# Reordering the first mixer of a two-layer encoder: pooled weights split, taps on TensorE, LayerNorm sums gathered tile by tile

## The chip, the cores and the metric

One program on one core of a Trainium2 chip. The metric is the device time of one execution in microseconds (us). TensorE is called PE, its weight loads PEld, VectorE DVE, ScalarE ACT, GpSimd POOL, SyncE SP.

## The reference, cut to what matters

SEQ is 512 positions, D_MODEL 1024. Layer 0 mixes with pooling and a 31-tap convolution, layer 1 with attention; each is followed by a LayerNorm, a gated feed-forward part and a gated embedding term. Only the mixer of layer 0 is touched by the change:

```python
def pool_conv_mixer(x, w_in, pool_w, pool_scale, dw_w, dw_b, cn_g, cn_b, w_out):
    u = x @ w_in                              # 1024 -> 512 pooled + 512 value + 512 gate
    a, b_val, b_gate = u[..., :512], u[..., 512:1024], u[..., 1024:]
    # 4 groups of 128 channels, trailing windows of 2, 4, 8, 16 positions
    d = stack([window_mean(a_g, w) - a_g for g, w in ...])
    y_a = einsum('bsgc,gcd->bsgd', d, pool_w).reshape(bsz, s, 512) * pool_scale
    glu = b_val * sigmoid(b_gate)
    h = causal_dwconv(glu, dw_w, dw_b)        # 31 taps for each of 512 channels
    y_b = silu(layer_norm(h, cn_g, cn_b))     # over the 512 channels
    return concatenate([y_a, y_b], axis=-1) @ w_out
# then, in layer i:
x = layer_norm(ALPHA * x + mix, ...)
ffn = conv_ffn(x, ...)
gate = sigmoid(x @ ple_w_gate[i] + ple_b_gate[i])
x = layer_norm(ALPHA * x + ffn + gate * (p[i] @ ple_w_proj[i]), ...)
```

## The kernel before

Everything is float32. Most products are made in three passes: each operand is split into a rounded high part and the rest (`split_into`, lines 77 to 79: ACT casts, DVE subtracts), and `mm3` (lines 81 to 84) multiplies high by high, high by low and low by high in the faster fp32r format. Weights stream through the class `Weights`: SP loads a unit of 128x1024 into `wraw` (3 buffers), `split` makes `whi` and `wlo` (7 buffers).

The mixer has its channels on partitions. Eight units of `w_in` give four pairs (value, gate) of 128 channels by 512 positions (`fm_tile`). `conv` makes `glu` from a pair, and `tick` deals out the taps: some as an ACT product with a POOL addition to `h` (lines 497 to 501), the others as a DVE multiply-add into an accumulator in PSUM (lines 505 and 507). A tile closes when DVE adds both (line 512). POOL's additions read the products `pr`, of which there are 4 buffers; ACT waits for POOL when they are full.

Meanwhile PE makes the pooled channels in `group` (line 569), plain fp32 products of `xr` and `wa`, which are not split; then the embedding product `pp` of the first half with the split embedding `pth`, then `window` (lines 580 and 584), the second half of `pp`, the pooled matrix `w_pool`, and the first half of the output projection. The channel LayerNorm comes when all four tiles `h` are closed: a product with `ones` gives the mean (line 677), DVE subtracts it, ACT squares, one-column products give the variance (line 690), POOL the inverse root, a diagonal product spreads it (line 700), DVE multiplies (line 703), and ACT applies Silu.

`mix_to_gate` then finishes the output projection for the second half of the channels, token tile by token tile (`r_77` to `r_80` are the four residual tiles): `residual` adds the product to `r` (line 344), statistics follow (311 to 317), two DVE operations per half apply the norm (324 and 325), and PE transposes the tile (line 336).

A scheduler orders the instructions of the mixer and the first feed-forward part from its own estimates; each engine then runs its list in order. So an instruction that waits holds up all behind it in its engine's list.

Of the kernel before, what the change touches and what calls it, by code (L numbers as in the profile page):

```python
# [9 lines left out]
F32 = mybir.dt.float32  # L10
# [5 lines left out]
P = 128  # L16
# [23 lines left out]

NOSYNC = mybir.DependencyInfo(mybir.DependencyClass.NoSync, mybir.DependencyReason.DATA)
# [17 lines left out]
def trunk(ctx, tc, x, xt, pt, cols, w_in, w_pool, w_mo, w_qk, w_v, w_o, relb, rows, w_up, w_dn, w_pp, w_pg, out):  # L59
# [8 lines left out]
    psp = ctx.enter_context(tc.tile_pool(name="psp", bufs=4, space=PSUM))  # L68

    def psa():  # L70
        return psp.tile([P, 512], F32, tag="a", name="psa")

    def psb():
        return psp.tile([P, 512], F32, tag="b", name="psb")
# [26 lines left out]
    order = [w_in[u] for u in range(8)] + [w_pp[0], w_pp[1], w_pool] + [w_mo[u] for u in range(8)]  # L101
# [17 lines left out]
    class Weights:  # L119
# [19 lines left out]
        def split(self, cuts=None):  # L139

            raw, n = self.raw[len(self.parts)]
            hi = wp.tile([P, 1024], F32R, tag="whi", name="whi")
            lo = wp.tile([P, 1024], F32R, tag="wlo", name="wlo")
# [45 lines left out]
    def fm_tile(a):  # L189
        o = psa()  # L190
        for _ in fm_gen(o, a):
            pass
        return o
# [99 lines left out]
    wa = big.tile([P, 4, D], F32, tag="a1h", name="wa")  # L293
    A1 = [None, big.tile([P, 8, 512], F32R, name="a1l")]
# [160 lines left out]
    with tc.tile_pool(name="mix", bufs=1, reuse_waits="tile") as mp:  # L455
# [24 lines left out]
        pool.memset(ones, 1.0 / 512.0)  # L480
# [6 lines left out]
        bg, convs, hs = deque(), deque(), []  # L487

        def tap(on_pool):


            k, np_, nd, c, glu, h, acc = convs[0]
            w = col(C_DW + c * TAPS + k)
            src = glu[:, k : k + S]
            if on_pool:
                if np_ == 0:
# [5 lines left out]
                np_ += 1  # L502
            else:
                if nd == 0:
                    vec.tensor_scalar(acc, src, w, col(C_DWB + c), op0=ALU.mult, op1=ALU.add)
                else:
                    vec.scalar_tensor_tensor(acc, src, w, acc, op0=ALU.mult, op1=ALU.add)
                nd += 1
            convs[0] = (k + 1, np_, nd, c, glu, h, acc)
            if k + 1 == TAPS:  # L510
                convs.popleft()
                bg.append(lambda: vec.tensor_tensor(h, h, acc, op=ALU.add))
# [11 lines left out]
        def conv(c, pv, pg):  # L524
# [6 lines left out]
            hs.append(h)  # L531
            convs.append((0, 0, 0, c, glu, h, psb()))
# [25 lines left out]


        am = (A1[1][:, 0:4, :], A1[1][:, 4:8, :])  # L560

        def group(t):

            ts = slice(t * P, (t + 1) * P)
            o = psa()
# [50 lines left out]
        for c in range(1, 4):  # L616
# [8 lines left out]
            if c == 1:  # L625
                nc.sync.dma_start(wa[:, 0, :], w_in[8])
# [360 lines left out]
```

## Time and profile before

| | |
|---|---|
| median of 3 runs | 1257.72 us (1254.5 to 1258.06) |
| the profiled execution | 1257.47 us, of which its span is 1255.8 us |
| busy: PE, PEld, DVE, ACT, POOL | 97%, 79%, 57%, 39%, 14% of the span |
| the first 100 us alone: PE, DVE, POOL | 87.7, 88.7, 79.1 us busy |

The busy shares are means over the span. The mixer is the first 160 us or so, and there DVE and POOL are nearly as busy as PE, which they are not later.

### The profile page before, as it was taken

The page shows a single profiled execution, that of the slowest core. Times are in us where ns is not written, and L with a number is a line of the kernel's source. Part 1 is how long each engine was busy: PE and PEld are TensorE (multiplying, and loading weights), DVE is VectorE, ACT ScalarE, POOL GpSimd, SP SyncE. Part 2 cuts the span into 40 slices and gives each one's busy share as a digit, 9 for nine tenths or more (in the row PEclk, how much of TensorE's full clock was granted, in tenths as well). Part 3 has the DMA queues.
Part 4 walks back from the last instruction along what each step waited for, and adds up shares of the span by engine and source line. Part 5 has one row for each costly group of instructions (what it writes and reads, how often), then busy time and mean ns, then how long its engine had stood idle before and what let it go on. Part 6 is the DMA issues. An engine that isn't in the chain of part 4 may idle for free.

```text
span 1255.8 us, 14245 instructions
## 1 busy us (share of the span) xinstructions
PE 1221.9 (97%) x5478; PEld 995.9 (79%) x5478; DVE 716.9 (57%) x1043; ACT 491.2 (39%) x745; POOL 175.6 (14%) x183
## 2 busy tenths in 40 slices
PE   8989999999999999999989999979999999999997
PEld 6638878888888888888878888868888888888886
DVE  7996586543444344447457777595544344434427
ACT  6764333431333133313357776222432233223320
POOL 5990040000000000004013233140000000000001
PEclk9999999999999999999999999999999999999999
DMA  9321123332222322333322222122322222223201
GB/s 364 137 67 67 51 101 107 129 101 101 93 92 101 101 94 90 101 101 101 134 84 76 96 82 67 67 101 85 134 91 94 101 101 98 87 101 101 96 22 67
DMA packets 36643, 125.11 MB, mean 100 GB/s; under 512 B 4064, under 2 KB 4448, under 8 KB 36576
## 3 DMA queue, kind: packets, MB, share of 16 engines
q1 hardware_dynamic: 36576, 124.20, 29.0%
q8 instruction: 43, 0.70, 0.2%
q14 instruction: 24, 0.20, 0.0%
HBM read 122.09 MB, written 2.10 MB: 99 GB/s over the span
## 4 chain that ended last, share of the span: by engine, by line
PE 86%; DVE 5%; POOL 5%; issue 2%; ACT 1%; DMA 1%; SPq 0%; DVEq 0%; POOLq 0%; ACTq 0%
PE psa L82 22%; PE psa L83 22%; PE psa L84 22%; PE psb L83 5%; PE psb L82 5%; PE psb L84 5%; POOL h L501 4%; PE psb L834 2%; DVE r L325 1%; DVE r L324 1%; PE psb L803 1%; PE psb L852 1%; PE psb L851 1%; PE psb L802 1%; POOL s L822 1%
## 5 line engine op out<-in xcount | busy, mean ns | idle before, releaser
L79 DVE TENSOR_TENSOR wlo<-wraw,whi 128x1024 fp32r<-128x1024 f32 (+3 forms) x191 | 239.3, 1254 | 328.7 <-ACT whi L78 322.6
L78 ACT CAST whi<-wraw 128x1024 fp32r<-128x1024 f32 (+2 forms) x203 | 211.8, 1043 | 460.9 <-PE psa L83 229.0
L82 PE MATMUL psa<-a0h,whi 128*128 128x512 f32 x896 | 351.0, 393 | 2.4 <-ACT whi L78 1.2
L84 PE MATMUL psa<-a0h,wlo 128*128 128x512 f32 x896 | 349.4, 390 | 2.0 <-DVE wlo L79 2.0
L83 PE MATMUL psa<-a0l,whi 128*128 128x512 f32 x896 | 349.6, 390 | 0.0
L82 PEld LDWEIGHTS psa<-a0h,whi 128*128 128x128 f32 x896 | 168.8, 188 | 38.4 <-ACT whi L78 2.2
L84 PEld LDWEIGHTS psa<-a0h,wlo 128*128 128x128 f32 x896 | 168.7, 188 | 38.2 <-DVE wlo L79 2.8
L83 PEld LDWEIGHTS psa<-a0l,whi 128*128 128x128 f32 x896 | 168.8, 188 | 34.7 <-DVE a0l L79 0.4
L319 POOL TENSOR_TENSOR rs<-ve,nhalf 128x1 f32<-128x1 f32 x16 | 15.0, 937 | 505.7 <-DVE ve L317 505.7
L411 DVE TENSOR_TENSOR hr<-t,psa 128x512 f32<-128x512 f32 x44 | 30.3, 689 | 86.0 <-PE psa L84 83.1
L501 POOL TENSOR_TENSOR h<-h,pr 128x512 f32<-128x512 f32 x47 | 71.1, 1526 | 6.0 <-ACT pr L500 3.7
L822 POOL TENSOR_TENSOR s<-s,rc 128x512 f32<-128x512 f32 (+1 forms) x64 | 47.8, 779 | 155.9 <-DVE rc L818 117.1
L82 PE MATMUL psa<-whi,a0h 128*128 128x512 f32 x160 | 63.7, 398 | 0.0
L82 PE MATMUL psa<-whi,a1h 128*128 128x512 f32 x160 | 63.0, 394 | 0.0
L83 PE MATMUL psb<-wlo,a1h 128*128 128x512 f32 x160 | 63.0, 394 | 0.0
L82 PE MATMUL psb<-whi,a1h 128*128 128x512 f32 x160 | 62.9, 393 | 0.0
L408 ACT ACTIVATE t<-t 128x512 f32<-128x512 f32 x44 | 27.9, 633 | 89.1 <-DVE t L407 89.1
L84 PE MATMUL psa<-whi,a0l 128*128 128x512 f32 x160 | 62.6, 391 | 0.0
L83 PE MATMUL psa<-wlo,a0h 128*128 128x512 f32 x160 | 62.5, 391 | 0.0
L83 PE MATMUL psa<-wlo,a1h 128*128 128x512 f32 x160 | 62.3, 389 | 0.0
L84 PE MATMUL psb<-whi,a1l 128*128 128x512 f32 x144 | 56.1, 398 | 0.0
L84 PE MATMUL psa<-whi,a1l 128*128 128x512 f32 x144 | 55.9, 389 | 0.0
(196 smaller groups left out, 1744.6 us busy)
## 6 DMA issues: line engine op xcount, KB each, us to landing
wraw<-in_w_up SPq DMA_DIRECT2D x88, 512.0 KB, 3.5
wraw<-in_w_dn SPq DMA_DIRECT2D x44, 512.0 KB, 3.5
wraw<-in_w_pg SPq DMA_DIRECT2D x16, 512.0 KB, 3.5
wraw<-in_w_qk SPq DMA_DIRECT2D x16, 512.0 KB, 3.5
wraw<-in_w_mo SPq DMA_DIRECT2D x8, 512.0 KB, 3.5
wraw<-in_w_v SPq DMA_DIRECT2D x8, 512.0 KB, 3.5
bt<-in_relb SPq DMA_DIRECT2D x16, 256.0 KB, 2.6
wraw<-in_w_o SPq DMA_DIRECT2D x8, 512.0 KB, 3.6
```

The source lines that it names most:

```text
L78: act.copy(hi, src)
L79: eng.tensor_tensor(lo, src, hi.bitcast(F32), op=ALU.subtract)
L82: pe.matmul(o, lhsT=ah, rhs=bh, start=first, stop=False)
L83: pe.matmul(o, lhsT=ah, rhs=bl, start=False, stop=False)
L84: pe.matmul(o, lhsT=al, rhs=bh, start=False, stop=last)
L319: pool.tensor_tensor(rs, ve, nhalf, op=ALU.pow)
L324: vec.scalar_tensor_tensor(r[t][:, c], r[t][:, c], mv[:, 0:1], self.g[:, c], op0=ALU.subtract, op1=ALU.mult)
L408: act.activation(t, t, AF.Gelu_apprx_tanh)
L411: vec.tensor_tensor(hr, t, pv, op=ALU.mult)
L501: pool.tensor_tensor(h, h, pr, op=ALU.add)
L822: pool.tensor_tensor(s[:, c], s[:, c], rc[:, b : b + 1].broadcast_to([P, n]), op=ALU.mult)
L834: pe.transpose(bank[:, n : n + P], s[:, SO[b] + j * P : SO[b] + (j + 1) * P], ident)
```

## The change

What is computed stays the same. In the order of the program:

- `make_bands` is issued ahead of the products; the Silu table is loaded once by a tiny activation.
- The four pooled units of `w_in` come through `Weights` and are split into `wa[0]` and `wa[1]`; `group` uses three passes, with the already split input `A0`.
- Taps 0 and 1 of each tile are products of PE with a diagonal matrix `dt` that ACT makes (`seed`); DVE then adds its taps to that accumulator.
- For tiles 2 and 3 `seed` also subtracts the channel mean of tile 0 with a product by `nmean`; `shift` does it for tiles 0 and 1 afterwards.
- The windows come right behind the groups, then `w_pool`, then half of the output projection's first half; the embedding product comes behind these.
- The LayerNorm's sums of `h` and of its square are one-column products made tile by tile (`sums`) between pieces of the embedding product. Mean and inverse root are both spread by diagonal products, and DVE multiplies and subtracts.
- The PSUM banks go by three tags (`a` and `c` with 2, `b` with 4).

```diff
-    order = [w_in[u] for u in range(8)] + [w_pp[0], w_pp[1], w_pool] + [w_mo[u] for u in range(8)]
+    order = [w_in[u] for u in range(12)] + [w_pool, w_mo[0], w_mo[1], w_pp[0], w_pp[1]] + [w_mo[u] for u in range(2, 8)]
...
+        def seed(n):
+            c, glu = n["c"], n["glu"]
+            n["acc"] = bank("c")
+            for k in range(PE_TAPS):
+                d = mp.tile([P, P], F32, tag="dt", name="dt", bufs=2)
+                act.activation(d, ident, AF.Copy, scale=col(C_DW + c * TAPS + k))
+                last = k == PE_TAPS - 1 and c < 2
+                pe.matmul(n["acc"], lhsT=d, rhs=glu[:, k : k + S], start=k == 0, stop=last)
+            if c >= 2:
+                pe.matmul(n["acc"], lhsT=nmean, rhs=hs[0], start=False, stop=True)
+            if c == 3:
+                bg.append(lambda: shift(0))
...
+        def close(n):
+            c, h = n["c"], n["h"]
+            vec.scalar_tensor_tensor(h, h, col(C_DWB + c), n["acc"], op0=ALU.add, op1=ALU.add)
+            hs.append(h)
+            if c == 1:
+                shift(1)
+
+        def shift(c):
+            sh = bank("a")
+            pe.matmul(sh, lhsT=nmean, rhs=hs[0], start=True, stop=True)
+            vec.tensor_tensor(hs[c], hs[c], sh, op=ALU.add)
...
             for k in range(KD):
-                lhs = xr[k // 2][:, H[k % 2]][:, ts]
-                pe.matmul(ov, lhsT=lhs, rhs=wa[:, :, k * P : (k + 1) * P], start=k == 0, stop=k == KD - 1)
-            split_into(am[0][:, t, :], am[1][:, t, :], o)
+                ks = slice(k * P, (k + 1) * P)
+                mm3(ov, A0[0][:, k, ts], A0[1][:, k, ts], wa[0][:, :, ks], wa[1][:, :, ks], k == 0, k == KD - 1)
+            a = mp.tile([P, 2, S], F32R, tag="pp", name="am", bufs=4)
+            split_into(a[:, 0, :], a[:, 1, :], o)
...
+        def sums(c):
+            sq = mp.tile([P, S], F32, tag="sg", name="sq", bufs=2)
+            act.activation(sq, hs[c], AF.Square)
+            for n, a in enumerate((sq, hs[c])):
+                for t in range(NT):
+                    i = n * NT + t
+                    pe.matmul(
+                        pvr[:, i : i + 1],
+                        lhsT=a[:, t * P : (t + 1) * P],
+                        rhs=mcol,
...
-        for c in range(4):
-            vec.tensor_tensor(hs[c], hs[c], pm, op=ALU.subtract)
...
+        both = []
+        for n in range(2):
+            if n:
+                vec.tensor_tensor(mean, mean, rs, op=ALU.mult)
+            dg = mp.tile([P, S], F32, tag="sg", name="dg", bufs=2)
+            v = mean if n else rs
...
         for c in range(4):
-            vec.tensor_tensor(hs[c], hs[c], rstd, op=ALU.mult)
+            vec.tensor_tensor(hs[c], hs[c], both[0], op=ALU.mult)
+            vec.tensor_tensor(hs[c], hs[c], both[1], op=ALU.subtract)
```

Three places in the engines' lists. The first is the start of the taps on DVE, in the kernel before from the first `glu` on:

```order
L529 TENSOR_TENSOR glu<-psa,sg 128x512
L505 TENSOR_SCALAR psb<-glu,cst 128x512
L507 SCALAR_TENSOR_TENSOR psb<-glu,cst,psb 128x512 x3
L79 TENSOR_TENSOR wlo<-wraw,whi 128x1024
L507 SCALAR_TENSOR_TENSOR psb<-glu,cst,psb 128x512 x2
```

And in the changed one:

```order
L578 TENSOR_TENSOR glu<-psa,sg 128x512
L88 TENSOR_TENSOR wlo<-wraw,whi 128x1024
L543 SCALAR_TENSOR_TENSOR psc<-glu,cst,psc 128x512
L88 TENSOR_TENSOR wlo<-wraw,whi 128x1024
L543 SCALAR_TENSOR_TENSOR psc<-glu,cst,psc 128x512 x5
```

Four taps that stood between `glu` and the first split now stand behind it, since they add to a bank that PE's seed fills.

The second is DVE around the windows in the changed kernel (`am` are the split group results, `a1l` on `psa`, `psb` the split windows, L553 a closing tile, L561 a shift):

```order
L543 SCALAR_TENSOR_TENSOR psc<-glu,cst,psc 128x512 x2
L88 TENSOR_TENSOR am<-psb,am 128x512
L553 SCALAR_TENSOR_TENSOR h<-h,cst,psc 128x512
L543 SCALAR_TENSOR_TENSOR psc<-glu,cst,psc 128x512
L561 TENSOR_TENSOR h<-h,psa 128x512
L543 SCALAR_TENSOR_TENSOR psc<-glu,cst,psc 128x512 x3
L88 TENSOR_TENSOR am<-psb,am 128x512
L543 SCALAR_TENSOR_TENSOR psc<-glu,cst,psc 128x512
L88 TENSOR_TENSOR a1l<-ptr,a1h 128x512 x2
L543 SCALAR_TENSOR_TENSOR psc<-glu,cst,psc 128x512 x2
L561 TENSOR_TENSOR h<-h,psa 128x512
L543 SCALAR_TENSOR_TENSOR psc<-glu,cst,psc 128x512 x4
```

The next row is the first split window, so eleven taps stand between the split of the third group and that of the first window. In the kernel before the embedding product and its splits stood between groups and windows.

The third is DVE in `mix_to_gate`, before:

```order
L344 SCALAR_TENSOR_TENSOR r_78<-r_78,psa 128x512
L315 BN_AGGR mv<-st 128x2
L311 BN_STATS st<-r_78 128x6
L317 TENSOR_SCALAR ve<-mv 128x1
L324 SCALAR_TENSOR_TENSOR r_77<-r_77,mv,g 128x512 x2
L315 BN_AGGR mv<-st 128x2
L325 SCALAR_TENSOR_TENSOR r_77<-r_77,rs,b 128x512 x2
```

And in the changed kernel:

```order
L357 SCALAR_TENSOR_TENSOR r_78<-r_78,psa 128x512
L324 BN_STATS st<-r_77 128x6
L324 BN_STATS st<-r_78 128x6
L328 BN_AGGR mv<-st 128x2 x2
L330 TENSOR_SCALAR ve<-mv 128x1
L337 SCALAR_TENSOR_TENSOR r_77<-r_77,mv,g 128x512 x2
L330 TENSOR_SCALAR ve<-mv 128x1
L337 SCALAR_TENSOR_TENSOR r_78<-r_78,mv,g 128x512 x2
L357 SCALAR_TENSOR_TENSOR r_79<-r_79,psc 128x512
L338 SCALAR_TENSOR_TENSOR r_77<-r_77,rs,b 128x512 x2
```

The last step of `r_77`, for which PE's transposes wait, now stands behind work on `r_78` and behind the residual of `r_79`. The PE list behind these transposes is the same in both kernels, and so are the lists of the feed-forward parts and the attention.

## Rows read from the trace of the kernel before

**Rows 1.** The page: span, busy time, the chain that ended last.

```profile
span 1255.8 us, 14245 instructions
PE 1221.9 (97%) x5478; PEld 995.9 (79%) x5478; DVE 716.9 (57%) x1043; ACT 491.2 (39%) x745; POOL 175.6 (14%) x183
PE 86%; DVE 5%; POOL 5%; issue 2%; ACT 1%; DMA 1%; SPq 0%; DVEq 0%; POOLq 0%; ACTq 0%
```

**Rows 2.** PE's waits from 0 to 200 us: total, times, longest.

```profile
PE psa L82 <- DVE a1l L79: 4.4, 2, 3.5
PE psa L336 <- DVE r L325: 2.4, 1, 2.4
...
PE psa L84 <- DVE wlo L79: 2.0, 2, 1.2
PE psa L82 <- ACT whi L78: 1.2, 1, 1.2
...
PE psa L84 <- DVE pth L79: 0.7, 2, 0.5
```

**Rows 3.** Stretches: length, busy per engine, granted clock, DMA share, GB/s.

```profile
94.40:102.40 8.00, 8.00 (x50) 7.68 (x51) 8.00 (x12) 3.29 (x5) 1.42 (x2) 0.79 0.07 17
...
126.00:130.00 4.00, 4.00 (x12) 3.14 (x13) 1.04 (x5) 0.00 (x0) 1.02 (x1) 0.57 0.00 0
...
174.10:178.00 3.90, 3.87 (x14) 3.45 (x15) 3.87 (x8) 2.44 (x3) 0.93 (x1) 0.56 0.15 56
```

**Rows 4.** DVE's groups by shape, 20 to 110 us.

```profile
L507 DVE SCALAR_TENSOR_TENSOR psb<-glu,cst,psb 128x512 f32<-128x512 f32 x69 | 48.4, 748 | 0.3
L79 DVE TENSOR_TENSOR wlo<-wraw,whi 128x1024 fp32r<-128x1024 f32 x13 | 22.6, 1739 | 4.8 <-ACT whi L78 4.8
```

**Rows 5.** DVE in order of time: start, length, what, how many.

```profile
20.62 0.81 DVE L505 TENSOR_SCALAR psb<-glu,cst 128x512 f32<-128x512 f32 x1
...
47.96 1.21 DVE L79 TENSOR_TENSOR wlo<-wraw,whi 128x1024 fp32r<-128x1024 f32 x1
...
94.23 4.70 DVE L507 SCALAR_TENSOR_TENSOR psb<-glu,cst,psb 128x512 f32<-128x512 f32 x7
98.84 0.68 DVE L512 TENSOR_TENSOR h<-h,psb 128x512 f32<-128x512 f32 x1
...
105.92 0.69 DVE L512 TENSOR_TENSOR h<-h,psb 128x512 f32<-128x512 f32 x1
```

**Rows 6.** POOL in order of time, its first additions.

```profile
22.05 62.08 POOL L501 TENSOR_TENSOR h<-h,pr 128x512 f32<-128x512 f32 x39 [3.25 <-ACT pr L500]
```

**Rows 7.** PE in order of time, to the end of the groups.

```profile
24.73 0.39 PE L83 MATMUL psa<-a0l,whi 128*128 128x512 f32 x1
25.86 0.50 PE L84 MATMUL psa<-a0h,wlo 128*128 128x512 f32 x1 [0.73 <-DVE wlo L79]
...
40.13 0.39 PE L82 MATMUL psa<-a0h,whi 128*128 128x512 f32 x1
...
55.79 27.63 PE L569 MATMUL psa<-wa,xr 128*128 128x512 f32 x64
```

**Rows 8.** PE in order of time, the longest wait and the one-column products.

```profile
94.37 0.50 PE L82 MATMUL psa<-whi,pth 128*128 128x512 f32 x1 [3.54 <-DVE a1l L79]
...
122.93 3.18 PE L690 MATMUL psa<-ones,sq 128*128 128x1 f32 x28
```

**Rows 9.** ACT in order of time, its first table load.

```profile
0.79 1.28 ACT L475 ACT_TABLE_LOAD   x1 [0.79 <-PEq L979]
```

**Rows 10.** DVE in order of time, in `mix_to_gate`.

```profile
155.07 0.69 DVE L344 SCALAR_TENSOR_TENSOR r<-r,psa 128x512 f32<-128x512 f32 x1
...
157.90 1.36 DVE L325 SCALAR_TENSOR_TENSOR r<-r,rs,b 128x512 f32<-128x512 f32 x2
```

**Rows 11.** PE in order of time, the first and the third transposed tile.

```profile
158.65 1.32 PE L336 MATMUL psa<-ident,r 128*128 128x128 f32 x8
...
174.13 1.97 PE L336 MATMUL psa<-ident,r 128*128 128x128 f32 x8 [2.37 <-DVE r L325]
```

More of the change, by code (lines that the diff above doesn't have):

```diff
@@ L1 @@
 from collections import deque
-from itertools import chain
+from itertools import chain, cycle
 import concourse.bass as bass
@@ L623, in trunk @@
             conv(c, pv, pg)
[L624 to L627 removed]
+        ptr = mp.tile([P, 2, S], F32, name="ptr")
+        nc.sync.dma_start(ptr, pt[0].rearrange("p (k t) -> p k t", k=2))
         for t in range(NT):
             nc.sync.dma_start(r[t], x[t * P : (t + 1) * P, :])
+        eps_t2 = sm.tile([P, 1], F32, tag="e2", name="eps_t2", bufs=1)
+        for _ in POOLED:
+            W.take()
+            W.free()
         for t in range(NT):
             group(t)
+            if t == 0:
+                act.activation(eps_t2, eps_t, AF.Silu)
             tick(*TICK)
@@ L652, in trunk @@
+            W.free()
+            if h == 0:
+                while bg or convs:
+                    tick(2, 1)
+                for c in range(min(3, len(hs)), 4):
+                    pass
             W.pump()
-            if h == 0:
-                A1[0] = big.tile([P, 8, 512], F32R, tag="a1h", name="a1h")
-                for g in range(NW):
-                    window(g)
         W.auto = True
-        while bg or convs:
-            tick(2, 1)
-        y = A1[:]
-        wpl = W.take()
@@ L691, in trunk @@
-        ve = sm.tile([P, NT], F32, tag="nm", name="ve4")
-        vec.tensor_scalar(ve, pvr[:, :NT], EPS, None, op0=ALU.add)
+        done = 3
+        for c in range(done, 4):
+            sums(c)
+        mean = sm.tile([P, NT], F32, tag="nm", name="mean")
+        vec.tensor_copy(mean, pvr[:, NT : 2 * NT])
+        sqm = sm.tile([P, NT], F32, tag="sqm", name="sqm")
+        vec.scalar_tensor_tensor(sqm, mean, -1.0, mean, op0=ALU.mult, op1=ALU.mult)
+        ve = sm.tile([P, NT], F32, tag="ve4", name="ve4")
@@ L693, in trunk @@
+        vec.scalar_tensor_tensor(ve, pvr[:, :NT], EPS, sqm, op0=ALU.add, op1=ALU.add)
         rs = sm.tile([P, NT], F32, tag="rc", name="rs4")
         pool.tensor_tensor(rs, ve, nhalf.broadcast_to([P, NT]), op=ALU.pow)
-        next(first)
-        dg = mp.tile([P, S], F32, tag="sg", name="dg", bufs=2)
-        for t in range(NT):
-            vec.tensor_scalar(dg[:, t * P : (t + 1) * P], ident, rs[:, t : t + 1], 512.0, op0=ALU.mult, op1=ALU.mult)
-        rstd = psa()
-        pe.matmul(rstd, lhsT=ones, rhs=dg, start=True, stop=True)
@@ L701, in trunk @@
-        next(first)
+        both = []
[4 more added lines that the diff above has]
+            v = mean if n else rs
+            for t in range(NT):
+                vec.tensor_scalar(dg[:, t * P : (t + 1) * P], ident, v[:, t : t + 1], None, op0=ALU.mult)
+            b = bank("c")
+            pe.matmul(b, lhsT=ones, rhs=dg, start=True, stop=True)
+            both.append(b)
```

178 lines of the change are left out of this document (102 added, 76 removed).

## The prediction

> **What bounds the kernel now.** I read the page first, then PE's waits, then DVE and POOL in order of time in the mixer. PE is busy for 97% of the span and holds 86% of the chain that ended last [rows 1], so outside the mixer time is PE work, and the lists behind the mixer are equal in both kernels. Only the first 180 us can differ. There PE waits in four places [rows 2]: 3.2 us for weights being split (2.0 for DVE, 1.2 for ACT), 5.1 us at the embedding product (4.4 for the split group results, 0.7 for `pth`), and 2.4 us in `mix_to_gate` for `r_79`. PE slows behind a long wait: the granted clock is 0.79 over the 8 us behind the wait of 3.54, and 0.56 behind the wait of 2.37 [rows 3, 8, 11]. It is also 0.57 behind the one-column products [rows 3]. The full clock is 2.4 GHz, the lower level 1.2. What PE waits for is DVE, which from 20.62 to its last closing tile at 105.92 has almost no gap [rows 5].
>
> **PE's work.** A product of 512 columns in fp32r takes (55.79 - 40.13) / 69 = 0.227 us [rows 7], with 69 products between the two rows. In plain fp32 it shows as two records of 27.63 / 64 = 0.432, so 0.864 [rows 7].
> - Groups: 32 fp32 products (27.6) become 96 at 0.227 (21.8): -5.8.
> - Eight diagonal products: +6.9. Four products with `nmean`: +3.5. The mean's four products with `ones` go: -3.5. A second spreading product: +0.9.
> - One-column products: 16 become 32. One is two records, and 28 of those take 3.18 [rows 8], so 0.22 each: +3.5.
>
> The sum is +5.5 us: PE gets more work, not less. Windows, embedding product, `w_pool` and output projection keep their counts.
>
> **DVE's work up to the last closing tile.** A tap takes (98.84 - 94.23) / 7 = 0.66 [rows 5]. Of 124 taps before, DVE did 73; of 116 it now does 67, and POOL 45 additions for 47: -4.0. The four splits of pooled weights come on top. A 1024-column split takes 1.21 alone [rows 5], but in the mean of this stretch 1.74 [rows 4], so +7.0 by the mean; the bounds are 4.8 (always alone) and 9.7 (each waits as long as it runs). Two shifts add 1.3. The scheduler also puts ahead of the last closing tile the four subtractions behind `w_pool` (2.6) and two splits (2.4) that stood behind it. At the start, DVE's first tap waits for the seed, which on PE stands behind unit 2 of `w_in`. That unit ends at 25.0 [rows 7], so the seed's 1.7 us end near 26.6. DVE, which began its taps at 20.62 [rows 5], has only one split to do until then: about 4 us idle, some 3 of which it spent idle further on before, so +1. In all 105.9 - 4.0 + 7.0 + 1.3 + 2.6 + 2.4 + 1 = 116 for the last closing tile, 10 us later. PE reaches the sums of the fourth tile only near 122, so this in itself costs nothing: the embedding product and half of the output projection cover it.
>
> At one place the Trainium skill speaks against the change. The row shows a split of 1.21 alone and 1.74 on average beside POOL's additions [rows 4, 5]. The page "SBUF — State Buffer", section "Who interferes with whom", says that a DVE instruction with two SBUF inputs and a GpSimd one that reads SBUF share a port under an exclusive lock, so that the later one is fully blocked. By it each of the four new splits could at worst wait for a whole addition, and blocks additions as well. The mean in the rows lies between that and no contact, and the sum goes by the mean.
>
> **PE in order of time in the changed kernel.** The early waits go: ACT's cast of unit 5 now stands behind 10 products instead of 13, and POOL's pace of 62.08 / 39 = 1.59 per addition [rows 6] sets when these can be made. PE starts the groups at 55.8 - 3.2 + 3.5 (two seeds) + 0.3 = 56.4. The 0.3 is for a second table load at the start: one takes 1.28 [rows 9], most of it before the first inputs; bounds 0 and 1.3.
>
> Groups (21.8), the third seed and three `nmean` products (4.3) and the first window pieces (0.8) bring PE to 83.3. It then needs the second and third group split. DVE has by then to do, from 20.6: 4.2 idle, 15 splits (26.1) and a half one (1.1), 41 taps (27.1), and seven short operations at about 0.6 (4.2); that gives 83.3, and some 84.8 with the dearer early taps, since the mean over all is 0.75 [rows 4]. A wait of 1 to 2 us.
>
> Behind it PE does the last seed, `nmean` and the other windows in 7.4 us, to about 92.2. DVE needs for the eleven taps (7.3) and seven short operations (4.3) 11.6 us until the first split window, 96.4, and 3.1 more until the fourth (two taps, three splits), 99.5. PE has 14 products (3.2) for that time. So PE passes this place at 99.6 instead of 83.3 + 7.4 + 3.2, with 5.7 us of waits in all. What is late next is `w_pool`'s results, but the embedding product and tile-by-tile order fill that.
>
> The half clock behind these waits falls partly into the next wait; I take 0.8 (bounds 0 and 1.7, the latter from 0.21 of 8 us [rows 3]) against the 1.7 that go with the old wait.
>
> To the first transposes: +5.5 - 3.2 - 5.1 - 1.7 + 5.7 + 0.3 + 0.8 = +2.3.
>
> **`mix_to_gate`.** Before, DVE had `r_77` ready as PE came to its transposes at 158.65 (residual of `r_78` at 155.07, last step of `r_77` at 157.90 [rows 10, 11]). Now two statistics, both first norm steps of `r_78` and the residual of `r_79` stand ahead of that last step. From the end of `r_78`'s sums, 12 products (2.7 us) ahead of the transposes: 0.25 to start, residual 0.6, two statistics 1.2, aggregation and epsilon 0.4, four norm steps 2.7, residual 0.6, one last step 0.7 = 6.4. So PE waits 6.4 - 2.7 = 3.7. In return `r_79` is ready in time: its steps end some 12 us after the first transposes would have started and PE wants it some 16 to 19 after. The wait of 2.4 goes [rows 11], and the half clock moves from one place to the other. Net +1.3.
>
> **Sum.** 2.3 + 1.3 = +3.6 on the profiled 1257.5 of which 1255.8 is span; the LayerNorm's half clock (0.43 of 4 us = 1.7 [rows 3]) may or may not go, since the one-column products now come in pieces of under 2 us: I take a third of it as gained, -0.6. Hence +3.0. The profiled execution and the median of 1257.7 differ by 0.2; the forecast is **1260.5 us**. A difference under 0.3%, 3.8 us, is what a measurement of this kernel cannot tell from none.
>
> **The rivals.**
> 1. *The waits go altogether* (faster). If collisions with POOL cost little, 15 splits at 1.21 instead of 1.74 bring DVE 8 us forward: both waits at the windows (5.7) and their half clock (0.8) vanish, and the LayerNorm's too (1.1 more): 1260.5 - 7.6 = 1253. For it: POOL has two additions fewer. Against: rows 4. It decides from a mean split of 1.4.
> 2. *ACT holds the group results back* (slower). ACT's casts of the last three group results stand behind products that wait for POOL; the second is behind 41 of them, so behind addition 37, at 22 + 37 x 1.59 = 81, in time. Four more splits than before hold POOL too. At 1.75 per addition the third cast, behind addition 38, comes at 88.5 and its split at 89.5, 4.7 after the 84.8 above, and the windows, their splits and all behind move by that: 1265. With the half clock in full at both new waits (2.6), 1267. It decides from 1.65 per addition.
> 3. *The seeds do not free DVE*: that DVE's work does not fall is already in the sum. Were the seed's four microseconds of idle time fully made up by shorter queues later, it would be -3: 1257.5, no change.
>
> Chances: the forecast with its neighbour 3, within 1255 to 1264.5, 0.50; rival 1 in part or whole 0.21; rival 2 in part or whole 0.29. The range that leaves out 2 in 10 is 1253 to 1267. The forecast stands close to the 0.3% border at 1261.5, so of its half I put 0.36 within and 0.14 above; with a small part of the rivals: faster 0.20, same 0.42, slower 0.38.
>
> **What would show it right or wrong.** In the changed profile: group products at 0.227; PE starting them near 56 with no waits for `whi` or `wlo`; PE waiting for `am` and `a1l` near 85 and 95, in all about 6 us; the last closing tile near 116 with no PE wait behind it; a wait of 3 to 4 us at the transposes of `r_77` and none at `r_79`. Wrong would be a mean split clearly off 1.74, POOL's pace off 1.6, or `r_77` in time.

## The result, and the profile after

The changed kernel takes 1272.18 us (median of 4, 1270.3 to 1272.39) against 1257.89 for the kernel before beside it: a ratio of 1.0115, 95% interval 1.0093 to 1.0136. It is slower by some 14 us, where 3 were forecast and 1267 was the upper end of the range. The page of the profiled execution (span, busy time of the engines, shares of the chain that ended last):

```profile
span 1270.4 us, 14431 instructions
...
PE 1234.9 (97%) x5560; PEld 1012.6 (80%) x5560; DVE 723.6 (57%) x1050; ACT 496.8 (39%) x757; POOL 177.7 (14%) x183
...
PE 86%; POOL 5%; DVE 4%; ACT 1%; issue 1%; DMA 1%; SPq 0%; DVEq 0%; POOLq 0%
```

Beside [rows 1], PE is busy for 13 us more and the span is 14.6 longer; POOL holds as much of the chain as before. PE's waits in the first 220 us (engine, what it does at which line, what it waits for, total, times, longest):

```profile
PE psb L491 <- ACT warm L488: 3.9, 1, 3.9
PE psc L519 <- DVE h L553: 3.8, 1, 3.8
PE psa L632 <- DVE h L561: 3.6, 1, 3.6
PE psc L349 <- DVE r L338: 3.5, 1, 3.5
PE psa L560 <- DVE am L88: 1.5, 1, 1.5
PE psb L92 <- DVE a1l L88: 0.3, 1, 0.3
```

Of [rows 2], the waits for split weights, for `pth` and for `r_79` are gone, as forecast. Three of 3.5 to 3.8 us stand in their place: for tile 0's closing (L553) ahead of the third tile's diagonal products, for a shift (L561) ahead of the fourth window, and for `r_77`. Behind each of them the granted clock is low (the 0.65, 0.57 and 0.72 near the end of each row; PE is hardly idle in these stretches):

```profile
69.00:77.00 8.00, 7.56 (x15) 3.79 (x16) 6.50 (x7) 6.10 (x9) 7.69 (x5) 0.65 0.50 187
101.00:109.00 8.00, 7.70 (x25) 5.76 (x26) 8.00 (x13) 5.02 (x9) 0.00 (x0) 0.57 0.00 0
172.00:178.00 6.00, 5.99 (x23) 4.74 (x24) 6.00 (x11) 2.61 (x4) 2.08 (x2) 0.72 0.00 0
```

That costs 0.35 x 8 + 0.43 x 8 + 0.28 x 6 = 7.9 us, and 8.5 with a first row that holds its stretch whole (from 66 on). Before there were two such stretches behind waits, 3.4 us in all [rows 3]. The one behind the one-column products, 1.7 us, is there in both kernels.

From the start of the span to the first feed-forward activation the kernel before takes 222.14 us and the changed one 232.85. PE's time splits into three parts: idle (length less busy), time lost to the lower clock (length times what the granted clock lacks to 1), and the rest, which I call work. The rows for all but the first 20 us, of before:

```profile
20.00:222.14 202.14, 191.03 (x796) 144.19 (x795) 157.76 (x211) 99.29 (x138) 86.02 (x56) 0.97 0.32 110
```

and of after:

```profile
20.00:232.85 212.85, 200.20 (x881) 159.58 (x880) 164.67 (x218) 103.92 (x148) 88.01 (x54) 0.95 0.30 105
```

The first 20 us add 3.5 and 3.9 of idle time at full clock. Over 200 us a clock of two digits is good to 1 us only, so the lost part in this table, and in what follows, is summed from narrow windows, each around one stretch at the lower level:

| to the first feed-forward activation | idle | lost to the clock | work | sum |
|---|---|---|---|---|
| before | 14.6 | 5.1 | 202.4 | 222.1 |
| after | 16.5 | 10.2 | 206.1 | 232.8 |
| forecast of the difference | -1.0 | -1.5 | +5.5 | +3.0 |
| measured difference | +1.9 | +5.1 | +3.7 | +10.7 |

Another 3.6 us come behind it: from that activation to the last `hr` of the last feed-forward part, before takes 982.7 us and after 986.3, with the same products in the same order. Split in the same way, these 3.6 us are 2.4 of work, 1.7 lost to the clock and -0.5 of idle time.

### The profile page after: what moved, and what is told of

Same layout as the page of the kernel before. It is cut to its first block, busy times and chain, and to the rows that moved or that the text cites. A ratio compares the mean times of both kernels' runs of the same rounds, so it can differ in the third digit from the quotient of the medians.

```text
span 1270.4 us, 14431 instructions
## 1 busy us (share of the span) xinstructions
PE 1234.9 (97%) x5560; PEld 1012.6 (80%) x5560; DVE 723.6 (57%) x1050; ACT 496.8 (39%) x757; POOL 177.7 (14%) x183
## 4 chain that ended last, share of the span: by engine, by line
PE 86%; POOL 5%; DVE 4%; ACT 1%; issue 1%; DMA 1%; SPq 0%; DVEq 0%; POOLq 0%
PE psa L91 11%; PE psa L92 11%; PE psa L93 11%; PE psc L91 11%; PE psc L93 11%; PE psc L92 11%; PE psb L92 5%; PE psb L93 5%; PE psb L91 5%; POOL h L540 4%; PE psb L923 2%; PE psb L892 1%; PE psb L940 1%; PE psb L941 1%; PE psb L891 1%
## 5 line engine op out<-in xcount | busy, mean ns | idle before, releaser
L88 DVE TENSOR_TENSOR wlo<-wraw,whi 128x1024 fp32r<-128x1024 f32 (+2 forms) x191 | 239.0, 1253 | 341.8 <-ACT whi L87 335.4
L87 ACT CAST whi<-wraw 128x1024 fp32r<-128x1024 f32 (+1 forms) x203 | 211.4, 1042 | 464.9 <-PE psb L93 118.5
L91 PE MATMUL psa<-a0h,whi 128*128 128x512 f32 x440 | 174.3, 396 | 0.0
L92 PE MATMUL psa<-a0l,whi 128*128 128x512 f32 x440 | 172.4, 392 | 0.0
L93 PE MATMUL psa<-a0h,wlo 128*128 128x512 f32 x440 | 172.2, 391 | 0.0
L91 PE MATMUL psc<-a0h,whi 128*128 128x512 f32 x416 | 162.5, 391 | 0.0
L93 PE MATMUL psc<-a0h,wlo 128*128 128x512 f32 x416 | 162.0, 389 | 0.0
L92 PE MATMUL psc<-a0l,whi 128*128 128x512 f32 x416 | 161.9, 389 | 0.0
L92 PEld LDWEIGHTS psa<-a0l,whi 128*128 128x128 f32 x440 | 83.2, 189 | 17.7 <-DVE a0l L88 0.4
L93 PEld LDWEIGHTS psa<-a0h,wlo 128*128 128x128 f32 x440 | 83.2, 189 | 17.5
```

Of the source, the lines that this page charges most:

```text
L87: act.copy(hi, src)
L88: eng.tensor_tensor(lo, src, hi.bitcast(F32), op=ALU.subtract)
L91: pe.matmul(o, lhsT=ah, rhs=bh, start=first, stop=False)
L92: pe.matmul(o, lhsT=ah, rhs=bl, start=False, stop=False)
L93: pe.matmul(o, lhsT=al, rhs=bh, start=False, stop=last)
```

## The experiments

Ratios are to the kernel before on the same chip; the changed kernel's is 1.0115, and 0.0010 is 1.26 us.

### What is lost behind the mixer

**e4_tags.** Two PSUM tags in the kernel before.

```diff
-        return psp.tile([P, 512], F32, tag="a", name="psa")
+        return psp.tile([P, 512], F32, tag=next(turns), name="psa")   # turns = cycle("aacc"), 2 banks each
```

> The kernel before, with one part of the change alone: the four PSUM banks of tag a become two of tag a and two of tag c taken in the order a, a, c, c. Behind the mixer the changed kernel lost 3.6 us more although its lists there are the same but for these tags. Theory A (the tags cost nothing, and what was lost behind the mixer has another cause): 1256 to 1260, no change. Theory B (the two rings make PE wait later on in the feed-forward parts or the attention): 1261 to 1263.

Ratio 1.0056 (1.0038 to 1.0075), slower as theory B has it, but not where B has it: 8.6 us are lost in the mixer and 2 to 3 regained later. With two tags the scheduler puts PE's transposes of `r_77` behind the last tile's part of the output projection and those of `r_78` right behind them:

```profile
168.73 1.11 PE L337 MATMUL psa<-ident,r 128*128 128x128 f32 x4 [3.89 <-DVE r L326]
171.49 1.11 PE L337 MATMUL psa<-ident,r 128*128 128x128 f32 x4 [1.64 <-DVE r L326]
```

The DVE steps that these wait for take 5.58 us for two, beside two weight splits on POOL; apart from such splits two take 1.36 [rows 10]:

```profile
165.85 5.58 DVE L326 SCALAR_TENSOR_TENSOR r<-r,rs,b 128x512 f32<-128x512 f32 x2
```

```profile
165.65 5.24 POOL L80 TENSOR_TENSOR wlo<-wraw,whi 128x1024 fp32r<-128x1024 f32 x2
```

In the changed kernel the transposes stand a product tile apart, as before. So the tags are a way to lose time, not the way in which it was lost here.

**e5_align and e12_before_moved.** In e5 the changed kernel's displacement of 160 bytes is made 256, a multiple of 128; in e12 the kernel before is given the 160.

```diff
-        eps_t2 = sm.tile([P, 1], F32, tag="e2", name="eps_t2", bufs=1)    # e5, in the changed kernel
+        eps_t2 = sm.tile([P, 32], F32, tag="e2", name="eps_t2", bufs=1)
...
+        pool.memset(sm.tile([P, 40], F32, tag="pad", name="pad", bufs=1), 0.0)    # e12, in the kernel before
```

> The changed kernel with one small tile made 128 bytes long instead of 4, so that everything allocated behind it in SBUF moves by 96 bytes per partition; no instruction changes. In the changed kernel the operand tiles hh and hl of the feed-forward parts' middle chunk start 160 bytes further on than before, at a multiple of 32 bytes and no longer of 128, and their products follow each other every 0.2343 us instead of 0.2289; 384 products make 2.1 us. Theory A (the address makes the difference): 0.2289 again, and the time falls by 2 to 3 us, to about 1269.5. Theory B (the banks psb and psc that they write, or DVE's work beside them, make it): still 0.2343, and 1271 to 1273.

> The kernel before with a small unused tile of 160 bytes ahead, so that the tiles behind it start where they start in the changed kernel: hh and hl of the feed-forward parts at a multiple of 32 bytes and not of 128. Lists of instructions are the same but for one short POOL instruction at the start. Theory A (the addresses cost what the changed kernel lost behind the mixer): their products at 0.2343 us instead of 0.2289, and the time rises by 2 to 4 us, to 1259 to 1261. Theory B (the spacing comes from something else in the changed kernel): 0.2289, no change.

e5: 1.0076 (1.0052 to 1.01), 4.9 us less than the changed kernel, whose interval it just touches. e12: 1.0039 (1.0024 to 1.0053), 4.9 us more than the kernel before, and its whole interval lies above 1. Theory A both times, by more than it said. Products of `hh`, start and length; first before, 32 products apart, (431.58 - 424.26) / 32 = 0.2288 us each:

```profile
424.26 0.39 PE L83 MATMUL psa<-wlo,hh 128*128 128x512 f32 x1
...
431.58 0.39 PE L82 MATMUL psa<-whi,hh 128*128 128x512 f32 x1
```

In the changed kernel, also 32 apart, 0.2341:

```profile
424.28 0.40 PE L92 MATMUL psb<-wlo,hh 128*128 128x512 f32 x1
...
431.77 0.40 PE L91 MATMUL psb<-whi,hh 128*128 128x512 f32 x1
```

In e12, 31 apart, 0.2345, with the instructions of before:

```profile
424.49 0.40 PE L82 MATMUL psb<-whi,hh 128*128 128x512 f32 x1
...
431.76 0.40 PE L83 MATMUL psa<-wlo,hh 128*128 128x512 f32 x1
```

384 such products make some 2 us. From the first feed-forward activation to the last `hr`, e5 takes 982.4 us (before 982.7) and e12 985.6 (after 986.3). But not all of this is the addresses. PE's work in that part is 971.1 to 972.1 us in the eight kernels with `hh` where the changed kernel has it and 968.1 to 969.3 in the ten with `hh` at a multiple of 128, e10 among them; the time lost to the clock there is 1.7 to 5.1 us in both groups, 5.1 in e10. The clock near 660 us (third number from the right) shows it, in the kernel before, in the changed one, and in e10:

```profile
650.00:670.00 20.00, 19.17 (x97) 16.46 (x98) 11.74 (x26) 13.44 (x32) 5.93 (x10) 0.91 0.24 78
```

```profile
650.00:670.00 20.00, 16.98 (x71) 14.04 (x70) 10.86 (x29) 12.84 (x29) 4.04 (x6) 0.83 0.24 82
```

```profile
650.00:670.00 20.00, 16.93 (x79) 14.31 (x78) 10.27 (x29) 11.60 (x27) 6.67 (x10) 0.83 0.25 72
```

So of the 3.6 us behind the mixer the addresses are some 2.4, and 1.7 is a clock that does not go with them. Over all executions, spans times granted clocks differ by 3.0 us between e12 and the kernel before and by 3.4 between the changed kernel and e5 (estimates from the span and clock of each execution; the second pair ran on different chips). So some 3 of the 4.9 us are shown to be the addresses; that the rest, lost to the clock, is theirs too is not shown.

**e16_moved64.** e12 with 16 elements in place of 40.

> The kernel before with an unused tile of 64 bytes ahead, so that hh and hl start at 64 bytes past a multiple of 128, where all the other operands of these products start (whi, wlo, a0h, a0l, a1h, a1l). Theory A (only starts that are no multiple of 64 cost): products of hh at 0.2289 us or less, and 1254 to 1258, no change. Theory B (only a multiple of 128 is good): products above 0.2289, and the time between the kernel before and the one moved by 160 bytes, 1258 to 1261. Theory C (what counts is that both operands start at the same place within 128 bytes): 0.2266, and 1 us faster.

0.999 (0.9974 to 1.0007): no difference in time that can be told, which fits theory A and the 1 us of theory C. The products go as theory C says, 31 apart, 0.2268:

```profile
424.64 0.39 PE L82 MATMUL psa<-whi,hh 128*128 128x512 f32 x1
...
431.67 0.39 PE L83 MATMUL psa<-wlo,hh 128*128 128x512 f32 x1
```

### What is lost in the mixer

**e2_bank.** The fourth window in a bank that needs no shift to be read.

```diff
-            o = [pse() for _ in range(NW)]
+            o = [pse() for _ in range(NW - 1)] + [bank("b")]
```

> The changed kernel, with the fourth window in a PSUM bank of tag b, so that it no longer waits for the bank that the spreading product of tile 0's mean holds until DVE has read it (a PE wait of 3.6 us at 97.3 us). Theory A (the bank alone holds PE there): the wait is gone, the first w_pool product starts 3 to 4 us earlier, and with the half clock behind it the time falls by 4 to 5 us, to 1267 or 1268. Theory B (DVE and ACT are late by themselves, so that the split windows come no earlier): PE waits as long a little further on, for a1h or a1l, and the time falls by at most 1 us, 1271 to 1272.

1.0116 (1.0096 to 1.0137): no gain, theory B. The wait of 3.6 is gone, and PE waits for `am` and `a1h` instead, starting `w_pool` at 101.9 instead of 102.5:

```profile
88.59 2.00 PE L560 MATMUL psa<-h,nmean 128*128 128x512 f32 x2 [2.66 <-DVE am L88]
...
101.92 0.50 PE L91 MATMUL psa<-a1h,whi 128*128 128x512 f32 x1 [2.76 <-ACT a1h L87]
```

**e3_noshift and e6_seedbank.** Two ways to free the third tile's products: e3 leaves out all products with `nmean` and both shifts (unshifted variance), e6 gives the accumulator another bank.

```diff
-            if c >= 2:                                                    # e3
-                pe.matmul(n["acc"], lhsT=nmean, rhs=hs[0], start=False, stop=True)
...
-            n["acc"] = bank("c")                                          # e6
+            n["acc"] = bank("b" if c == 2 else "c")
```

> The changed kernel without the subtraction of tile 0's mean: four products with nmean (3.5 us of PE) and two DVE additions (1.4 us) go, the LayerNorm takes its variance from unshifted sums. Theory A (the third tile's diagonal products wait for DVE to close tile 0 because they take over the PSUM bank of its accumulator): the wait of 3.8 us at 65.7 stays within 1 us, the wait of 3.6 for the fourth window goes, and the time falls by 3.5 (products) and some 2 to 3 (wait, half clock), to about 1266. Theory B (they wait because their third product reads tile 0 itself): both waits go, with the half clock behind them, and the time falls by about 10 us, to 1262.

> The changed kernel, with the third tile's diagonal products written to a PSUM bank of tag b, so that they need not wait until DVE has closed tile 0 (a PE wait of 3.8 us at 65.7, and half clock behind it). They still wait for tile 0 through the product with nmean, which can stand later in PE's list. Theory A (PE's wait is a loss of its own): the wait is gone, and with the half clock behind it the time falls by 4 to 6 us, to about 1267. Theory B (the windows are held back by DVE and ACT, which do not get earlier): PE waits longer for am and a1h near 90 to 100, and only the half clock is gained: 1270 to 1272.

e3: 1.0142 (1.0119 to 1.0164), no gain although 3.5 us of PE are gone; both theories had less. The wait at the diagonal products stays, as theory A says (the bank holds them), PE waits longer for other things, `r_77` among them, and 13.7 us are lost to the clock, 3.4 more than in the changed kernel:

```profile
PE psc L349 <- DVE r L338: 5.2, 1, 5.2
...
PE psc L519 <- DVE h L549: 3.8, 1, 3.8
```

e6: 1.0089 (1.0066 to 1.0112). Its interval overlaps the changed kernel's, so the 3 us may be chance; and the wait is not gone, as theory A had it. The diagonal products come early, and the product with `nmean` behind them waits as long for the same closing:

```profile
56.15 1.88 PE L519 MATMUL psb<-glu,dt 128*128 128x512 f32 x4
...
69.58 1.74 PE L521 MATMUL psb<-h,nmean 128*128 128x512 f32 x2 [3.78 <-DVE h L553]
```

So bank and data both tie the third tile to tile 0's closing at 68.65, and to take one away is not enough.

**e7_pr6.** Six buffers of `pr` (the raw embedding moves into another tile to make room).

```diff
-                    pr = mp.tile([P, S], F32, tag="pr", name="pr", bufs=4)
+                    pr = mp.tile([P, S], F32, tag="pr", name="pr", bufs=6)
```

> The changed kernel with six buffers of products pr instead of four, so that ACT can run further ahead of POOL's additions (ACT waits 18.8 us for POOL between 20 and 130 us, and DVE 9.3 us for casts that stand behind these products on ACT). Theory A (ACT held by POOL is what makes the windows late): DVE's idle time for whi falls below 5 us, the windows come 3 to 5 us earlier, and the time falls by 2 to 5 us, to about 1268.5. Theory B (POOL's pace of 1.68 us per addition is the limit, and two more buffers only move the place where ACT waits): ACT's wait and the time stay, 1271 to 1273.

1.0111 (1.0084 to 1.0138): no gain, theory B. ACT's wait falls only to 12.6 us, from 18.8, and POOL's 45 additions take 75.4 us as in the changed kernel. Tile 0 closes at 60.3, so the third tile's products run without a wait, but PE then waits 6.4 us in one piece for `am` (the profiled execution is 4.9 us below this kernel's median):

```profile
61.22 1.88 PE L519 MATMUL psc<-glu,dt 128*128 128x512 f32 x4
...
85.34 2.07 PE L560 MATMUL psa<-h,nmean 128*128 128x512 f32 x2 [6.44 <-DVE am L88]
```

**e8_noseed and e9_noseed_pr6.** No products of PE for taps or mean (unshifted variance): `PE_TAPS = 0`, DVE's first tap with the bias as before, the closing a plain addition. e9 adds e5's and e7's edits.

> The changed kernel without any products of PE for the taps: no diagonal products, no product with nmean (12 products, 10.4 us of PE), all 31 taps again by DVE or ACT and POOL, and the LayerNorm's variance from unshifted sums. DVE gets 8 taps more and 2 additions less (+4 us), and starts its taps some 4 us earlier. Theory A (PE's list sets the time once the waits for the seeds are gone): the time falls by 8 us or more, to 1264 or less. Theory B (DVE's list up to the windows and the last closing tile sets it): PE waits longer at the windows, and the time falls by less than 4 us, to 1268 to 1274.

> The changed kernel with three edits together: no products of PE for the taps and the mean shift (unshifted variance), six buffers of pr, and the tiles behind the small pool at a multiple of 128 bytes again. What stays of the change: pooled weights split, new order of windows and embedding product, channel LayerNorm from gathered sums, PSUM tags. Theory A (the three losses are separate: 5 us for the seeds, 6 for ACT behind POOL, 4 to 5 for the addresses): the feed-forward part starts near 222 as before, and the time is 1255 to 1260. Theory B (seeds and pr buffers act on the same wait, PE's for the split group results, so that their gains overlap): a wait of 4 us or more for am stays, and the time is 1261 to 1265.

e8: 1.0083 (1.0062 to 1.0105), 4 us less than the changed kernel, with intervals that overlap; the median of 1266.9 lies between the theories. Of work it has some 193 us, 13.1 less, but 21.1 idle and 13.7 lost to the clock: PE waits 7.1 us for ACT's cast of `am` and then runs slowly (third number from the right):

```profile
80.00:100.00 20.00, 15.75 (x62) 13.64 (x63) 16.56 (x26) 16.12 (x27) 19.29 (x15) 0.58 0.06 23
```

e9: 1.0082 (1.006 to 1.0103), no less than e8. PE still waits 7.7 us for `am`, as theory B says, but the median of 1267.3 is above B's range too: 23.9 idle, 20.5 lost to the clock. Much of the work taken from PE comes back as waits and clock.

**e10_seedbank_pr6.** e5, e6 and e7 together.

> The changed kernel with three edits together: the third tile's diagonal products in a bank of tag b, six buffers of pr, and the tiles behind the small pool at a multiple of 128 bytes. Theory A (the gains of 3 us in the mixer for the bank, 6 for the buffers and 4 for the addresses add): first feed-forward activation near 224, time 1258 to 1260. Theory B (with six buffers tile 0 is closed in time, so that the bank gives nothing more): first feed-forward activation near 226.5, time 1262 to 1265.

1.0039 (1.0021 to 1.0056), 9.5 us less than the changed kernel; the median of 1261.3 lies between the theories. Its profile is of the longest of 12 executions, 4.9 us above the median; in it the first feed-forward activation comes at 228.5, later than either theory has it, with 14.4 us idle and 8.5 lost to the clock. With e9 it shows that the diagonal products are worth having: e9 is e10 without them and without the product with tile 0's mean, and 5 us slower, although it has some 16 us less of PE's work; 12 us of that come back as lost clock and 9.5 as idle time.

**e14_plain.** e10 with the pooled weights unsplit: plain products of `xr` and `wa`, as in the kernel before, and splits of the windows behind the last window product.

> The kernel of e10 with the pooled products undone: plain fp32 products of unsplit weights (27.6 us of PE instead of 21.8), no casts and splits of the four pooled units; the split windows must wait for the last window product, since the group results lie where they go. Theory A (the splits of the pooled weights, 7 us of DVE, cost at PE's waits and half clock behind them about what the faster products give): within 2 us of e10, 1259 to 1263. Theory B (PE's work sets the time, as in the prediction's sum): 4 to 6 us slower than e10, 1265 to 1267.

1.0119 (1.0097 to 1.0142), 10 us slower than e10; both theories had less. Up to the feed-forward part work rises by 4.4 us, as in theory B, and the loss to the clock by 3.4 to 12.0, of which 9 lie in one stretch:

```profile
100.00:120.00 20.00, 19.27 (x74) 17.33 (x75) 13.41 (x20) 7.60 (x12) 0.00 (x0) 0.55 0.12 42
```

So the split groups pay, and DVE's four splits are not where the loss lies. Part of the 10 us may be the later splits of the windows, which this version needs.

**e11_before_pr6.** The kernel before with six buffers.

> The kernel before with six buffers of pr instead of four (half of the split embedding is kept in another tile for that, with no other change). Theory A (ACT held by POOL's additions, 17.3 us of waits, is behind PE's waits for weights and for the embedding product, 3.2 and 5.1 us): at least half of these go, and the time falls by 3 to 6 us, to 1252 to 1255. Theory B (in the kernel before DVE is late by itself): no change, within 2 us.

1.0016 (1.0 to 1.0032): no gain here either, theory B.

### The end of the mixer

**e1_order.** In `mix_to_gate` the residual of a tile stays behind the last norm step of the tile before.

```diff
             residual(t, 1, by.o[t], True)
+            if t:
+                tc.add_manual_dep(ins[n], last[t - 1], NOSYNC, reason="written order")
```

> The changed kernel, with one dependence added on DVE's list in mix_to_gate: the residual of a token tile may not stand ahead of the last norm step of the tile before it, so r_77's last step no longer stands behind the work on r_78 and the residual of r_79. Theory A (PE waits at the transposes of r_77, 3.5 us and some half clock behind it, because of that order): the wait shrinks to about 1 us, and the time falls by 2.5 to 4 us, to about 1269. Theory B (the wait only moves, to the transposes of r_78 or r_79): a wait of 2 us or more for r_78 or r_79 appears, and the time changes by under 1 us, 1271 to 1273.

1.0122 (1.0103 to 1.0141): no gain, theory B. PE waits 0.6 us for `r_77` and 3.8 for `r_79`, the tile behind `r_78`:

```profile
169.43 0.66 PE L349 MATMUL psc<-ident,r 128*128 128x128 f32 x4 [0.61 <-DVE r L338]
...
186.77 0.63 PE L349 MATMUL psc<-ident,r 128*128 128x128 f32 x4 [3.83 <-issue]
```

The reason is on DVE: the last steps of `r_78` take 5.70 us where those of `r_77` took 1.40,

```profile
168.63 1.40 DVE L338 SCALAR_TENSOR_TENSOR r<-r,rs,b 128x512 f32<-128x512 f32 x2
...
174.09 5.70 DVE L338 SCALAR_TENSOR_TENSOR r<-r,rs,b 128x512 f32<-128x512 f32 x2
```

and POOL does three weight splits just then:

```profile
173.88 8.16 POOL L88 TENSOR_TENSOR wlo<-wraw,whi 128x1024 fp32r<-128x1024 f32 x3
```

**e13_order_dve and e15_before_dve.** All weight splits on DVE (`W.eng = pool` becomes `W.eng = vec` in `pipeline`), in e10 with e1's order, and in the kernel before.

> The kernel of e10 (seed in another bank, six buffers of pr, addresses at 128), with two edits more: the order of DVE's norm steps of e1, and all weight splits on DVE, none on POOL. In e1 two norm steps of r_78 took 5.7 us instead of 1.4 beside a POOL split, and PE waited for r_78 instead of r_77. Theory A (POOL's splits hold DVE's steps up): steps of 0.7 us each throughout, no PE wait over 1 us in mix_to_gate, and 3 to 6 us less than e10, 1255 to 1258. Theory B (DVE has no room for four to eight splits of 1.2 us there): the waits come back for other tiles, within 2 us of e10, 1260 to 1263.

> The kernel before, with all weight splits on DVE and none on POOL. In the kernel before four POOL splits stretch six DVE steps of about 0.7 us to 2.5 to 2.9, in both layers, and PE waits 2.4 and 8.0 us for what follows. Theory A (these collisions cause the waits): 3 to 6 us faster, 1250 to 1253. Theory B (a split on DVE takes as much room as the collision did): within 2 us, 1254 to 1258.

e13: 1.0022 (1.0007 to 1.0038), 2 us less than e10 with overlapping intervals; the median of 1258.7 lies between the theories. Without POOL the two steps of `r_78` take their 1.41:

```profile
170.04 1.41 DVE L338 SCALAR_TENSOR_TENSOR r<-r,rs,b 128x512 f32<-128x512 f32 x2
```

PE still waits 3.0 us for a tile, `r_79`, since four splits of 1.2 us now stand on DVE. e15: 0.9996 (0.9976 to 1.0015), no difference, theory B. The collision is real, and no gain from its removal can be told.

**e17_best and e18_best64.** e13 without the early Silu and with the two rings of PSUM in turn (`cycle("ac")`); e18 also moves the tiles to 64 bytes past a multiple of 128.

> The kernel of e13 without the tiny early Silu (which stands first in ACT's list and costs a second table load) and with the two PSUM rings taken in turn, a, c, a, c. A version put together from what gained. Theory A (what is left of the loss is waits for which these edits make room): 1254 to 1257, level with the kernel before. Theory B (what is left is half clock behind PE's waits for am, and more PE work): within 1.5 us of e13, 1257 to 1260.

> The mended kernel of e17, with the tiles behind the small pool moved by 64 bytes more, so that hh and hl start at 64 bytes past a multiple of 128, as whi and wlo do. Instructions are the same. Theory A (the same place within 128 bytes is what counts, as in e16): products of hh at 0.2267 us, and 1 to 4 us less than e17, 1254 to 1257, level with the kernel before or faster than it. Theory B (e16's profile was a favourable one): 0.2289, no difference from e17.

e17: 1.001 (0.9998 to 1.0023), within 1.5 us of e13 as theory B says; e18: 1.0003 (0.9984 to 1.0021). The mended kernel is level with the kernel before and does not beat it. e18's products of `hh` are 0.2267 us apart, as theory A says, and its time cannot be told from e17's.

## Why the prediction was wrong

**Right.** PE's work: +5.5 forecast, +3.7 measured. PE started the groups at 55.99 (56.4 forecast), with products at 0.227. The waits for weights, for the embedding and for `r_79` went; `r_77` came late by 3.5 us (3.7 forecast). The windows' waits were 1.5 + 3.6 + 0.3 = 5.4 us (5.7 forecast). DVE's last closing came at 125.5, 9.5 us later than the forecast 116; that no wait of PE stands behind it is as said. In e1 and e4 DVE's norm steps last 2.8 us each beside POOL's splits instead of 0.7, and 0.7 with none on POOL (e13). The Trainium skill, page "SBUF — State Buffer", section "Who interferes with whom", has a DVE instruction with two SBUF inputs contend with a GpSimd instruction that reads SBUF, for a port pair under an exclusive lock; these rows agree with it. In the mixer the mean split in this kernel is as forecast for `wlo` and shorter for the new `wal`:

```profile
L88 DVE TENSOR_TENSOR wlo<-wraw,whi 128x1024 fp32r<-128x1024 f32 x14 | 24.1, 1727 | 9.4 <-ACT whi L87 9.3
L88 DVE TENSOR_TENSOR wal<-wraw,wah 128x1024 fp32r<-128x1024 f32 x4 | 5.9, 1468 | 0.0
```

**Where the miss lies.** Measured are +14.3 us instead of +3.0. Of the 11.3 between, 6.6 are the clock up to the feed-forward part (+5.1 for -1.5), 2.9 idle time there (+1.9 for -1.0), -1.8 work (+3.7 for +5.5), and 3.6 lie behind the mixer, where the forecast had nothing. The steps that failed, in turn:

**The first step that failed** stands ahead of the sum: "outside the mixer time is PE work, and the lists behind the mixer are equal in both kernels. Only the first 180 us can differ." The lists are equal, the addresses were not: the change allocates 160 bytes more ahead of the tiles of the later parts. Taking that back gave 4.9 us (e5) and giving it to the kernel before cost 4.9 (e12), some 3 of them in the pace of products. No row of the kernel before could have shown it; a listing of tile addresses would have shown the displacement, though not its price. Of the 3.6 us behind the mixer another 1.7 are clock, which comes and goes there whatever the addresses.

**The second: which case came about.** Without the displacement the change costs 1.0076 (e5), 1266 us, where rival 2 stood with 1265 to 1267, and not the forecast. Its markers came true, its price only in part. POOL's 45 additions took 75.58 / 45 = 1.68 us each, above the 1.65 from which it decides (1.59 was taken, from [rows 6]):

```profile
22.78 75.58 POOL L540 TENSOR_TENSOR h<-h,pr 128x512 f32<-128x512 f32 x45 [3.23 <-ACT pr L539]
```

ACT's casts of group results stand between products that wait for POOL; the third came at 89.20, where the rival had 88.5:

```profile
87.23 0.72 ACT L539 ACTIVATE pr<-glu,cst 128x512 f32<-128x512 f32 x1 [0.65 <-POOL h L540]
87.86 0.57 ACT L87 CAST am<-psa 128x512 fp32r<-128x512 f32 x1
88.46 0.69 DVE L88 TENSOR_TENSOR am<-psa,am 128x512 fp32r<-128x512 f32 x1 [1.59 <-ACT am L87]
88.58 0.72 ACT L539 ACTIVATE pr<-glu,cst 128x512 f32<-128x512 f32 x1 [0.15 <-POOL h L540]
89.20 1.12 PE L560 MATMUL psa<-h,nmean 128*128 128x512 f32 x2 [1.46 <-DVE am L88]
89.20 0.57 ACT L87 CAST am<-psb 128x512 fp32r<-128x512 f32 x1
```

Its split followed at 90.38 (84.8 in the forecast's sum, 89.5 in the rival's):

```profile
68.65 0.73 DVE L553 SCALAR_TENSOR_TENSOR h<-h,cst,psc 128x512 f32<-128x512 f32 x1
...
90.38 0.68 DVE L88 TENSOR_TENSOR am<-psb,am 128x512 fp32r<-128x512 f32 x1
...
125.53 0.75 DVE L553 SCALAR_TENSOR_TENSOR h<-h,cst,psc 128x512 f32<-128x512 f32 x1
```

PE's wait there is for the second group's split, whose cast the rival held to be in time, and it is 1.5 us. Up to `w_pool` PE waits 3.8 + 1.5 + 3.6 + 0.3 = 9.2 us, where the forecast has 5.7 and the rival 10.4; in e7, without the 3.8, it is still 8.5, 6.4 of them for `am`. So the late group results set PE's arrival as the rival says, but that the time fits as well is partly luck, since the rival gave the clock less than it took. What the runs add is that two more buffers do not mend it (e7, e11). That POOL's pace is then the limit fits this, but no run made POOL faster.

**The third: the term for the clock.** "I take 0.8" for the half clock behind the new waits, and -0.6 for the LayerNorm. Measured: +5.1 in place of -1.5, the largest miss of all. Each of the three waits of 3.5 to 3.8 us was followed by 1.7 to 3.4 us lost, 8.5 in all; the bound of 1.7 for one stretch was carried over as a bound for all. The stretch behind the one-column products stayed, so the -0.6 did not come.

**The fourth: a wait that was not seen.** "Groups (21.8), the third seed and three `nmean` products (4.3)" gave the third seed no wait. It takes over the bank of tile 0's accumulator and adds tile 0's mean, so it stands in PE's list behind a closing on DVE (68.65; PE was there at 65.7). The order showed where it stands; whose bank it takes was not asked. Its 3.8 us are more than the 2.9 by which idle time missed the forecast. To free the bank or the data alone left the wait in place (e3, e6), and where other edits removed it (e7), PE waited for `am` instead. So it is not shown to have cost anything by itself.

**What stays open.** The parts of the mixer's loss cannot be priced one by one: single edits there (e1, e2, e3, e7) gave nothing that can be told, e6 perhaps 3 us, and e10's three edits together gave 9.5 us, where e5, e6 and e7 alone gave 4.9, 3.3 and 0.5. How the scheduler reorders with each edit is part of every such run. Nor is it settled why the clock falls behind one wait and not behind another of the same length (below).

## What to carry to other kernels

When an engine off the path sets the pace, a wait that is removed comes back elsewhere: count idle time, time lost to the clock and work over the whole stretch, and look for a change in the sum, not in one wait. Ask of each product that is moved early whose PSUM bank it takes and who frees it. Compare the addresses of the tiles in both versions before blaming equal instruction lists.

## What the runs showed of the hardware

- **The start address of an operand changes the speed of a product.** fp32r products of 512 columns with `whi` and `wlo` at 64 bytes past a multiple of 128 (places follow from the kernels' tile sizes, the displacements from the edits): 0.2267 to 0.2268 us each with `hh` and `hl` at 64 too (e16, e18), 0.2288 with them at 0 (before), 0.2341 to 0.2345 at 32 (after, e12). 160 bytes of displacement cost a kernel of 1256 us some 3 us in this way, and 4.9 by its median (1.0024 to 1.0053). Where the difference arises in the engine no run shows.
- **The granted clock does not follow from a wait alone.** e5 has the instruction lists of the changed kernel and the same wait of 3.5 us ahead of `r_77`, but the full clock behind it, where the changed kernel had 0.72:

```profile
172.00:178.00 6.00, 5.73 (x29) 4.70 (x30) 6.00 (x12) 3.57 (x5) 1.74 (x2) 1.00 0.00 0
```

  Likewise the kernel before, e16 and e12 have the same lists but for one instruction on POOL, and lost 5.1, 6.8 and 8.5 us to the clock up to the feed-forward part in their profiled executions.

- **PE work in a stretch with waits is partly free.** With 12 products fewer (e8) PE did some 13.1 us less work up to the feed-forward part, and 8.0 us of that came back, 4.6 as idle time and 3.4 as clock.
